# Transposes taken from a queue, one behind each wide product, in a hybrid decoder layer

## The chip, the cores and the metric

One core of a Trainium2 chip runs the whole layer. The metric is the device time of one execution in microseconds; three runs of each kernel are timed.

## The reference, cut to what matters

One layer for 2048 tokens behind 16 meta tokens, 1024 channels, four heads, in float32:

```
n = rmsnorm(h);  u, q, k, v = split(n @ w_in)
ya = pooling mixer of u (trailing means of 2, 4, 8, 16), w_pool
q, k = rmsnorm per head half (64 channels)
a  = softmax(q1 k1^T / 8) - lam * softmax(q2 k2^T / 8)      causal
yb = rmsnorm(a @ v) * 0.8
h  = h + [ya | yb] @ w_out
n  = rmsnorm(h);  u = n @ w_up            1024 x 5632
c  = causal depthwise conv of u (width 3) + b
h  = h + (silu(c_gate) * c_val) @ w_down
```

## The kernel before

Tokens go in 16 blocks of 128 (b = 0 to 15) and one of the 16 meta tokens (b = -1). Every float32 product is made from three products of split operands (hi with hi, hi with lo, lo with hi), which `mm3` writes out; each of them loads 128 columns of weights and streams 128 to 512 columns. A product here is called wide when it streams 256 or more.

TensorE contracts over partitions, so several operands are transposed first, each time 128 columns with the data as weights and the identity as what streams. A group of two to four such transposes fills one PSUM tile `pt`; then `split` empties it: ScalarE copies the hi part, VectorE subtracts to get lo. There are 1024 transposes, in four places:

- the norm's output `n` of each block, eight in two groups of four, by `transpose_split` (line 187) in the first stage. The result `nT` is used for head 0 and kept in DRAM for the other heads;
- q and k of each head and block, two, by `qk_store` (line 286). Their result goes by a transfer to `qk_d` in DRAM, and after every fourth block `load_kv` reads keys and values back;
- the mixed probabilities `p`, by `values` (lines 685 and 708), four to a group, for the products with v;
- the second norm's output `n`, eight by `out_finish` (line 987).

The stages: first, head 0's projection for all blocks together with the pooling mixer. Then attention of heads 0 to 3, score chunks (line 649, up to 512 keys) and products with v, woven with the projections of heads 1 to 3 and, for the last head, with the first half of the out projection. Then the second half of the out projection with the second norm, and behind it the feed-forward part, which holds more than half of the span. The first up-projection chunk, `first` (line 954, 72 products), is written ahead of the last `out_finish`.

A scheduler orders the instructions: each takes its place on its engine by its place in the program, by priorities, and by when the scheduler thinks that its operands are there. So products are used to fill what it takes for gaps. Transfers are all started by the queue SP in that order; one that waits holds up those behind it.

Of the kernel before, what the change touches and what calls it, by code (L numbers as in the profile page):

```python
# [76 lines left out]
def layer_kernel(  # L77
# [104 lines left out]
    def transpose_split(ps_pool, n, T, hi, lo):  # L182
        for half in range(2):
            pt = ps_pool.tile([P, 4, P], F32, name="pt")
            for j in range(4):
                kc = half * 4 + j
                nc.tensor.transpose(pt[:, j, :T], n[:T, kc * P:(kc + 1) * P], ident[:T, :T])  # L187
            split(pt[:, :, :T], hi[:, half * 4:half * 4 + 4, :T], lo[:, half * 4:half * 4 + 4, :T])
# [45 lines left out]
    def norm_block(b, ptr, g_row, h=None):  # L234
        T, pos = block(b)
        h = load_x(b) if h is None else h
        n = nrm.tile([P, D], F32, name="n")
        r = rms_rows(nrm, h[:T], T, "n1", n[:T])
        nc.vector.scalar_tensor_tensor(n[:T], h[:T], r, g_row[:T], ALU.mult, ALU.mult)
        pn, pc = pair_cols(b)  # L240
        if pn not in pairs:
            pairs[pn] = (nrm if pn % 2 else npa).tile([P, 2, KC, NM + 2 * P], F32R, name="nT", bufs=1)
        nT = pairs[pn][:, :, :, pc]
        transpose_split(ptr, n, T, nT[:, 0], nT[:, 1])
        nc.sync.dma_start(
            nT_d[b].rearrange("p a k t -> p (a k) t"),
            nT.rearrange("p a k t -> p (a k) t").bitcast(F32))
        return nT

    def qkv_block(h, b, nT, whi, wlo, ppm):  # L250
        T, pos = block(b)
        ps = ppm.tile([P, 512], F32, name="pm")
        mm3(ps[:T, :3 * P], [(nT[:, 0, kc, :T], nT[:, 1, kc, :T], whi[kc], wlo[kc]) for kc in range(KC)])
# [27 lines left out]
    def qk_store(h, b, qn, ps_pool, tag):  # L281
        T, pos = block(b)
        pt = ps_pool.tile([P, 4, P], F32, name=tag)
        qT = inp.tile([P, 2, 2, P], F32R, name="qT")
        for g in range(2):
            nc.tensor.transpose(pt[:, g, :T], qn[:T, g * P:(g + 1) * P], ident[:T, :T])
        split(pt[:, 0:2, :T], qT[:, :, 0, :T], qT[:, :, 1, :T])
        pn, pc = pair_cols(b)
        nc.sync.dma_start(
            qk_d[h][pn][:, :, :, pc].rearrange("p s a t -> p (s a) t"),  # L290
            qT[:, :, :, :T].rearrange("p s a t -> p (s a) t").bitcast(F32),
        )
# [98 lines left out]
    with tc.tile_pool(name="apm", bufs=4, space=PSUM, reuse_waits="tile") as ppm, \  # L391
# [44 lines left out]
        for b in range(-1, NB):  # L436
            nT = nTs.pop(0)
            if b == NB - 1:
                u_groups(NP - 1, (0, 1))
                u_groups(NP - 1, (2, 3))  # L440
# [186 lines left out]
    def scores(key, qs, n, ks, res):  # L627
        q0 = NM if n == 0 else 0
        for ib in range(2):
# [7 lines left out]
            for c in range(2):  # L637
                for ch in range(npc):
# [4 lines left out]
                    while c == 1 and live[1] >= P2_BUFS:  # L643
                        mix_next()
                    live[c] += 1
                    dst = ap.tile([P, 512], F32, name=f"p{c + 1}", bufs=P1_BUFS if c == 0 else P2_BUFS)[:, :k1 - k0]
                    pt[c].append(dst)
                    for a in range(2):
                        nc.tensor.matmul(  # L649
                            src, qs[:, c, a, q0 + ib * P:q0 + (ib + 1) * P], ks[:, c, k0:k1],  # L650
                            start=(a == 0), stop=(a == 1 and not diag))
                    if diag:
                        nc.tensor.matmul(
                            s_ps[:, k1 - k0 - P:k1 - k0], ident_bf, mask_bf, start=False, stop=True)
# [15 lines left out]
    def values(key, n, a, vs, vm):  # L670
# [18 lines left out]
        late = []  # L689

# [8 lines left out]
        for m in range(n + 1):  # L699
            pt = ptr.tile([P, 512], F32, name="pt")  # L700
            width = 512 if m < n else 3 * P
            for jj in range(2):
                j = 2 * m + jj
                for ib in range(2):
                    if j > 2 * n + ib:
                        continue
                    off = jj * QP + (ib if m < n or jj == 0 else 0) * P
                    nc.tensor.transpose(  # L708
                        pt[:, off:off + P], piece(a[ib], NM + j * P), ident)
            at = ap.tile([P, 2, 512], F32R, name="at", bufs=AT_BUFS)  # L710
            split(pt[:, :width], at[:, 0, :width], at[:, 1, :width])
            gone = [end for end in spans if end <= NM + 2 * (m + 1) * P]
            live[0] -= len(gone)
            spans = [end for end in spans if end > NM + 2 * (m + 1) * P]
            late.append((m, at))
            yield VLW * (1 - PSH)
            if len(late) > PV_LAG:
                products(*late.pop(0))
                yield VLW * PSH
        for m, at in late:  # L720
            products(m, at)
            yield VLW * PSH
# [52 lines left out]
    def project(h):  # L775
# [3 lines left out]

        def finish(b, qn):  # L780
            qk_store(h, b, qn, *((ppm, "pm") if QPM else (ptr, "pt")))
            if b > 0 and b % 4 == 3:
                part = b // 4
                if part == 0:
                    assert ended[0] >= (h - 1) * NP, (h, ended)
                    kvs[h] = alloc_kv(h)
                load_kv(h, part, kvs[h])
                parts.add((h, part))
# [11 lines left out]
        run_later(1 << 30)  # L800
        if h + 1 < H:
# [42 lines left out]
    def out_half(b, k0, base):  # L844
# [8 lines left out]
        for hf in range(2):  # L853
# [4 lines left out]
                for k in range(4)])  # L858
# [44 lines left out]
    def need(h, part):  # L903
        while (h, part) not in parts:
            if later:
# [13 lines left out]
    run_later(1 << 30)  # L919
    kv[1].release()  # L920
# [39 lines left out]
    with tc.tile_pool(name="os", bufs=2, **LEFT) as sp:  # L960
# [18 lines left out]
        def out_finish(b, n):  # L979
            T, pos = block(b)  # L980
            if b >= 7:
                n2T = sp.tile([P, KC, P], F32, name="n2T")
            for q in range(2):
                pt = ptr.tile([P, 512], F32, name="pt").rearrange("p (j t) -> p j t", t=P)
                for j in range(4):
                    kc = q * 4 + j
                    nc.tensor.transpose(pt[:, j, :T], n[:T, kc * P:(kc + 1) * P], ident[:T, :T])
                if b < 8:
                    t0 = max(0, pos - (NM - 4))
                    src = pt[:, :, T - 4:T] if b < 0 else pt  # L990
                    cols = slice(t0, t0 + (4 if b < 0 else T))
                    split(src, fnT[q][:, 0, :, cols], fnT[q][:, 1, :, cols])
                if b >= 7:
                    nc.scalar.copy(n2T[:, q * 4:q * 4 + 4], pt)  # L994
            if b >= 7:
                nc.sync.dma_start(n2_d[:, :, pos:pos + T].rearrange("k p t -> p k t"), n2T)
# [3 lines left out]
        for b in range(-1, NB):  # L1000
            n = out_block(b)
            if last is not None:
# [6 lines left out]
            last = (b, n)  # L1009
        first = up_products(0, load_up(0), ppx)  # L1010
        out_finish(*last)
    ppx.release()
# [122 lines left out]
```

## Time and profile before

| what | value |
|---|---|
| median of three runs | 2544.81 us (2540.98 to 2545.67) |
| span of the profiled execution | 2541.9 us |
| TensorE busy | 2492.5 us, 98% |
| VectorE, ScalarE, GpSimd busy | 62%, 37%, 16% |
| transfers | 314.32 MB, all on one core's 16 DMA engines |
| feed-forward part | from some 1060 us to the end |

The profiled execution is one more execution of the same program; of its time the profile gives the span from its first to its last instruction, and what lies around it is not shown. The span is 2.9 us below the median of the runs and inside their range. Times in rows are microseconds from the start of the span. Matmuls overlap and their ends are modelled, so the distance of two starts says what a product costs, not its duration.

### The profile page before, as it was taken

The page shows a single profiled execution, that of the slowest core. Times are in us where ns is not written, and L with a number is a line of the kernel's source. Part 1 is how long each engine was busy: PE and PEld are TensorE (multiplying, and loading weights), DVE is VectorE, ACT ScalarE, POOL GpSimd, SP SyncE. Part 2 cuts the span into 40 slices and gives each one's busy share as a digit, 9 for nine tenths or more (in the row PEclk, how much of TensorE's full clock was granted, in tenths as well). Part 3 has the DMA queues.
Part 4 walks back from the last instruction along what each step waited for, and adds up shares of the span by engine and source line. Part 5 has one row for each costly group of instructions (what it writes and reads, how often), then busy time and mean ns, then how long its engine had stood idle before and what let it go on. Part 6 is the DMA issues. An engine that isn't in the chain of part 4 may idle for free.

```text
span 2541.9 us, 35879 instructions
## 1 busy us (share of the span) xinstructions
PE 2492.5 (98%) x13614; PEld 2185.7 (86%) x13614; DVE 1564.3 (62%) x3106; ACT 948.0 (37%) x2270; POOL 410.5 (16%) x480
## 2 busy tenths in 40 slices
PE   8998999999989999999999999999999999999999
PEld 7997898888877887899999999998888888888887
DVE  7886898889798646454444444445554454445545
ACT  5544676667676434322221222223222122212221
POOL 1001555556575430000000000000000000000000
PEclk9999999999999999999999999999999999999999
DMA  9866767675655568911111111112611111111111
GB/s 274 257 204 202 216 202 213 202 225 175 226 159 159 188 197 273 292 55 48 42 34 50 50 50 50 42 50 83 207 50 42 50 50 37 39 50 50 50 34 66
DMA packets 320952, 314.32 MB, mean 124 GB/s; under 512 B 28188, under 2 KB 280012, under 8 KB 314636
## 3 DMA queue, kind: packets, MB, share of 16 engines
q1 hardware_dynamic: 320780, 312.03, 40.1%
q8 instruction: 107, 1.75, 0.3%
q14 instruction: 65, 0.53, 0.1%
HBM read 222.85 MB, written 89.13 MB: 123 GB/s over the span
## 4 chain that ended last, share of the span: by engine, by line
PE 90%; DMA 5%; DVE 3%; ACT 1%; issue 1%; POOL 0%; SPq 0%; ACTq 0%; DVEq 0%
PE pu L954 39%; PE pm L193 6%; PE pm L194 6%; PE pm L195 6%; PE pd L193 6%; PE pd L195 6%; PE pd L194 6%; PE s_ps L649 4%; PE pt L708 2%; DMA nTs<-nT_d 1%; PE o_ps L679 1%; PE o_ps L680 1%; PE o_ps L681 1%; DMA wraw<-in_w_in_dram 1%; PE pt L187 1%; PE pt L512 1%
## 5 line engine op out<-in xcount | busy, mean ns | idle before, releaser
L954 PE MATMUL pu<-fnT,uwh 128*128 128x344 f32 (+1 forms) x3520 | 807.1, 350 | 1.9 <-ACT n2T L994 1.9
L954 PEld LDWEIGHTS pu<-fnT,uwh 128*128 128x128 f32 x3520 | 617.6, 189 | 76.0 <-ACT n2T L994 2.1
L1090 DVE TENSOR_TENSOR acc<-pd,acc 128x512 f32<-128x512 f32 x368 | 252.8, 688 | 474.8 <-PE pd L195 474.4
L954 PE MATMUL pu<-fnT,uwl 128*128 128x344 f32 (+1 forms) x1760 | 453.7, 350 | 0.0
L179 ACT CAST uwh<-uraw 128x1024 fp32r<-128x1024 f32 x88 | 92.3, 1049 | 688.4 <-PE pu L954 677.3
L954 PEld LDWEIGHTS pu<-fnT,uwl 128*128 128x128 f32 x1760 | 312.0, 189 | 32.7
L193 PE MATMUL pd<-dwh,g 128*128 128x512 f32 x688 | 272.5, 396 | 3.0 <-DVE acc L1090 2.7
L195 PE MATMUL pd<-dwh,g 128*128 128x512 f32 x688 | 271.1, 394 | 0.0
L194 PE MATMUL pd<-dwl,g 128*128 128x512 f32 x688 | 270.9, 394 | 0.0
L656 ACT ACTIVATE p<-s_ps,nm 128x400 f32<-128x400 f32 (+4 forms) x352 | 211.6, 603 | 126.0 <-DVE nm L655 102.8
L180 DVE TENSOR_TENSOR uwl<-uraw,uwh 128x1024 fp32r<-128x1024 f32 x88 | 107.7, 1224 | 232.3 <-ACT uwh L179 230.5
L593 POOL TENSOR_SCALAR p<-p,fac 128x384 f32<-128x384 f32 (+4 forms) x164 | 219.5, 1353 | 102.9 <-DVE fac L588 72.9
L655 DVE TENSOR_REDUCE nm<-s_ps 128x1 f32<-128x400 f32 (+4 forms) x352 | 197.2, 566 | 57.0 <-PE s_ps L649 29.8
L649 PE MATMUL s_ps<-ks,qs 128*128 128x400 f32 (+4 forms) x704 | 196.3, 365 | 5.5 <-ACT p L656 3.6
L195 PEld LDWEIGHTS pd<-dwh,g 128*128 128x128 f32 x688 | 129.4, 188 | 30.9
L193 PEld LDWEIGHTS pd<-dwh,g 128*128 128x128 f32 x688 | 129.6, 188 | 29.9 <-DVE acc L1090 6.6
L193 PE MATMUL pm<-whi,nTs 128*128 128x384 f32 (+1 forms) x408 | 143.2, 353 | 10.4 <-DMA nTs<-nT_d 9.7
L194 PEld LDWEIGHTS pd<-dwl,g 128*128 128x128 f32 x688 | 129.3, 188 | 23.3
L179 ACT CAST g<-c 128x1026 fp32r<-128x1026 f32 (+1 forms) x44 | 46.2, 1050 | 261.5 <-DVE c L1070 162.0
L194 PE MATMUL pm<-wlo,nTs 128*128 128x384 f32 (+1 forms) x408 | 141.8, 348 | 0.1
L195 PE MATMUL pm<-whi,nTs 128*128 128x384 f32 (+1 forms) x408 | 141.4, 347 | 0.0
L649 PEld LDWEIGHTS s_ps<-ks,qs 128*128 128x128 f32 x704 | 117.0, 190 | 15.2 <-ACT p L656 8.2
(217 smaller groups left out, 4309.2 us busy)
## 6 DMA issues: line engine op xcount, KB each, us to landing
nTs<-nT_d SPq DMA_DIRECT2D x48, 1024.0 KB, 5.9
uraw<-in_w_up_dram SPq DMA_DIRECT2D x88, 512.0 KB, 3.9
draw<-in_w_down_dram SPq DMA_DIRECT2D x44, 512.0 KB, 4.0
nT_d<-nT SPq DMA_DIRECT2D x16, 1024.0 KB, 6.5
qk_d<-qT SPq DMA_DIRECT2D x64, 256.0 KB, 4.9
mt<-mix_d SPq DMA_DIRECT2D x32, 512.0 KB, 4.5
h_d<-xt SPq DMA_DIRECT2D x32, 512.0 KB, 5.2
qs<-qk_d SPq DMA_DIRECT2D x56, 256.0 KB, 4.4
```

The costliest lines, as they stand in the source:

```text
L179: nc.scalar.copy(hi, src)
L180: eng.tensor_tensor(lo, src, hi.bitcast(F32), ALU.subtract)
L193: nc.tensor.matmul(ps, a_hi, b_hi, start=(i == 0), stop=False)
L194: nc.tensor.matmul(ps, a_hi, b_lo, start=False, stop=False)
L195: nc.tensor.matmul(ps, a_lo, b_hi, start=False, stop=(i == n - 1))
L593: nc.gpsimd.tensor_scalar(a1, a1, fac[:, 0, ch:ch + 1], None, ALU.mult)
L649: nc.tensor.matmul(src, qs[:, c, a, q0 + ib * P:q0 + (ib + 1) * P], ks[:, c, k0:k1], start=(a == 0), stop=(a == 1 and not diag))
L655: nc.vector.tensor_reduce(nm[:, c, ch:ch + 1], src, AX.X, ALU.max, negate=True)
L656: nc.scalar.activation(dst, src, AF.Exp, bias=nm[:, c, ch:ch + 1], accum_out=ls[:, c, ch:ch + 1])
L708: nc.tensor.transpose(pt[:, off:off + P], piece(a[ib], NM + j * P), ident)
L954: nc.tensor.matmul(ps[:, bk, :wid], wt[:, kc], fnT[kc // 4][:, a, kc % 4, bk * w0:bk * w0 + wid], start=(kc == 0 and a == 0 and wt is wh), ...
L1090: nc.vector.tensor_tensor(acc[b][:, cs], ps, acc[b][:, cs], ALU.add)
```

## The change

Transposes are no longer issued where they are written. `turn` puts a group into the list `turning` with a function `end` for what follows it (the split, and the store or load behind that). `turn_one` issues the next transpose of the first group; the last of a group calls `end`. `mm3` with `wide` issues one behind each product: in the projections, in both halves of the out projection and, by a call of its own, behind each score product. With `tight` the next product is also tied behind that transpose for the scheduler; so it is for head 0's projection (`not h`) and the second half of the out projection (`k0 > 0`), not in attention. Places that need a result now empty the queue first (`turn_all`, `turned`).

```
+    def turn(pool, tag, steps, end):
+        group = dict(pool=pool, tag=tag, steps=list(steps), end=end, pt=None)
+        turning.append(group)
+        return group
+
+    def turn_one():
+        if turning:
+            group = turning[0]
+            if group["pt"] is None:
+                group["pt"] = group["pool"].tile([P, 512], F32, name=group["tag"])
+            out, in_, T = group["steps"].pop(0)
+            ins = nc.tensor.transpose(group["pt"][:, out:out + T], in_, ident[:T, :T])
+            if not group["steps"]:
+                turning.pop(0)
+                group["end"](group["pt"])
+            return ins
+        return None
...
-    def mm3(ps, pairs):
+    def mm3(ps, pairs, wide=False, tight=False):
...
-            nc.tensor.matmul(ps, a_hi, b_hi, start=(i == 0), stop=False)
-            nc.tensor.matmul(ps, a_hi, b_lo, start=False, stop=False)
-            nc.tensor.matmul(ps, a_lo, b_hi, start=False, stop=(i == n - 1))
+            for k, (a, b) in enumerate(((a_hi, b_hi), (a_hi, b_lo), (a_lo, b_hi))):
+                with tc.issue_after(turned.ins) if turned else nullcontext():
+                    ins = nc.tensor.matmul(ps, a, b, start=(i == 0 and k == 0), stop=(i == n - 1 and k == 2))
+                if wide:
+                    with tc.issue_after(ins.ins):
+                        turned = turn_one()
+                if not tight:
+                    turned = None
...
         for b in range(-1, NB):
             n = out_block(b)
+            turn_all()
             if last is not None:
                 out_finish(*last)
...
             last = (b, n)
+        turn_all()
         first = up_products(0, load_up(0), ppx)
         out_finish(*last)
+        turn_all()
```

In `values` the scores' PSUM and the p tiles (`live[0]`) are now given back when the group's last transpose is issued, and a score chunk that finds no free p tile issues transposes first.

What this makes of the order on the engines is seen at three places. The first is TensorE in head 0's projection, ahead of the products of a block (`pt<-ident,n` and `pt<-ident,qn` are transposes, `pm<-whi` and `pm<-wlo` products of the projection). Before:

```order
L187 MATMUL pt<-ident,n 128x128 x8
L286 MATMUL pt<-ident,qn 128x128 x2
L193 MATMUL pm<-whi_218,nT 128x384
L194 MATMUL pm<-wlo_219,nT 128x384
L195 MATMUL pm<-whi_218,nT 128x384
L193 MATMUL pm<-whi_223,nT 128x384
```

and in the change:

```order
L233 MATMUL pm<-whi_203,nT 128x384
L197 MATMUL pt<-ident,n 128x128
L233 MATMUL pm<-wlo_204,nT 128x384
L197 MATMUL pt<-ident,n 128x128
L233 MATMUL pm<-whi_203,nT 128x384
L197 MATMUL pt<-ident,n 128x128
L233 MATMUL pm<-whi_208,nT 128x384
L197 MATMUL pt<-ident,n 128x128
```

The eight and two transposes that stood ahead of the block's 24 products now stand behind its first ten products, one each.

The second is the queue SP where head 0 ends (`qk_d_7_82<-qT` is the last block's store of q and k, `nTs<-nT_d_60` the load of block 1 for head 1, `wraw` are weights of a later projection, `ks` reads the stored keys back, `qs` queries). Before:

```order
L217 DMA wraw<-in_w_in_dram 128x3x128 x3
L289 DMA qk_d_7_82<-qT 512x1x128
L794 DMA nTs<-nT_d_60 128x2048
L794 DMA nTs<-nT_d_61 128x2048
L307 DMA ks_360<-qk_d_7_82 64x2x256
L259 DMA v_d_108<-vt 16x256
L259 DMA v_d_108<-vt 128x256
L307 DMA ks_360<-qk_d_7_82 64x2x256
L544 DMA qs<-qk_d_2_77 64x2x512 x2
```

and in the change:

```order
L330 DMA qk_d_7_82<-qT 512x1x128
L260 DMA wraw<-in_w_in_dram 128x3x128
L352 DMA ks_330<-qk_d_7_82 64x2x256
L260 DMA wraw<-in_w_in_dram 128x3x128
L352 DMA ks_330<-qk_d_7_82 64x2x256
L593 DMA qs<-qk_d_2_77 64x2x512 x2
L853 DMA nTs<-nT_d_60 128x2048
```

The load of block 1 stood right behind the store; now two loads of ks, which wait for that store to land, and two of qs stand ahead of it, and two weight loads that stood before the store.

The third is TensorE at the end of the out projection (`pm<-ks,mt` and `pm<-vs,mt` are its products, `pu` those of the up projection; the last two groups of transposes are blocks 14 and 15). Before:

```order
L194 MATMUL pm<-vs_11323,mt 128x512
L195 MATMUL pm<-ks_11322,mt 128x512
L954 MATMUL pu<-fnT_13473,uwh 128x344 x3
L954 MATMUL pu<-fnT_13473,uwl 128x344 x3
L954 MATMUL pu<-fnT_13473,uwh 128x344 x3
L987 MATMUL pt<-ident,n_14431 128x128 x8
L954 MATMUL pu<-fnT_13473,uwh 128x344 x3
L954 MATMUL pu<-fnT_13473,uwl 128x344 x3
L954 MATMUL pu<-fnT_13473,uwh 128x344 x6
L954 MATMUL pu<-fnT_13473,uwl 128x344 x3
L954 MATMUL pu<-fnT_13473,uwh 128x344 x6
L954 MATMUL pu<-fnT_13473,uwl 128x344 x3
```

and in the change:

```order
L233 MATMUL pm<-vs_11300,mt 128x512
L233 MATMUL pm<-ks_11299,mt 128x512
L197 MATMUL pt<-ident,n_14431 128x128 x8
L197 MATMUL pt<-ident,n_14492 128x128 x8
L1017 MATMUL pu<-fnT_13472,uwh 128x344 x6
```

Between the last out product and the next chunk there were two bursts of eight with 9 and 24 up products around them; now there are the two bursts alone, and the 72 up products of that chunk stand earlier.

## Rows read from the trace of the kernel before

**Rows 1.** Table by stretches: window, its length, TensorE busy us (instructions), granted clock, DMA share, GB/s.

```profile
36.00:208.00 172.00, 172.00 (x1303) 1.00 0.82 239
...
250.00:712.00 462.00, 454.19 (x2857) 1.00 0.67 206
...
931.00:1060.00 129.00, 123.80 (x632) 1.00 0.83 259
```

**Rows 2.** List by line, TensorE: count | busy us, mean ns | idle before, releasers.

```profile
L708 PE MATMUL pt<-ident,p 128*128 128x128 f32 x544 | 85.6, 275 | 0.2
...
L187 PE MATMUL pt<-ident,n 128*128 128x128 f32 (+1 forms) x136 | 18.1, 275 | 10.1 <-DVE n L239 10.1
```

**Rows 3.** Timeline of TensorE, a burst of eight: start us, us, engine, line, operation.

```profile
1029.69 1.03 PE L987 MATMUL pt<-ident,n 128*128 128x128 f32 x8
1030.48 0.48 PE L194 MATMUL pm<-vs,mt 128*128 128x512 f32 x1
1030.80 0.39 PE L195 MATMUL pm<-ks,mt 128*128 128x512 f32 x1
```

**Rows 4.** Timeline of TensorE, a lone transpose in attention.

```profile
775.13 0.60 PE L649 MATMUL s_ps<-ks,qs 128*128 128x384 f32 x2
775.56 0.27 PE L708 MATMUL pt<-ident,p 128*128 128x128 f32 x1
775.59 0.47 PE L193 MATMUL pm<-ohi,mt 128*128 128x512 f32 x1
775.90 0.39 PE L194 MATMUL pm<-olo,mt 128*128 128x512 f32 x1
776.13 0.40 PE L195 MATMUL pm<-ohi,mt 128*128 128x512 f32 x1
```

**Rows 5.** Timeline of the queue SP, end of the first head.

```profile
223.93 0.56 SPq L289 DMA_DIRECT2D qk_d<-qT  x1
224.54 2.28 SPq L794 DMA_DIRECT2D nTs<-nT_d  x2
228.16 0.63 SPq L307 DMA_DIRECT2D ks<-qk_d  x1
...
230.81 1.23 SPq L544 DMA_DIRECT2D qs<-qk_d  x2
```

**Rows 6.** Timeline of TensorE, same place; in brackets the idle time before.

```profile
231.37 0.66 PE L193 MATMUL pm<-whi,nTs 128*128 128x384 f32 x1 [3.33 <-DMA nTs<-nT_d]
...
239.39 0.34 PE L194 MATMUL pm<-wlo,nTs 128*128 128x384 f32 x1
239.56 0.34 PE L195 MATMUL pm<-whi,nTs 128*128 128x384 f32 x1
```

**Rows 7.** Timeline of VectorE, last block of the out projection.

```profile
1050.87 0.69 DVE L859 TENSOR_TENSOR xt<-pm,xt 128x512 f32<-128x512 f32 x1 [2.03 <-PE pm L195]
...
1054.62 1.28 DVE L976 SCALAR_TENSOR_TENSOR n<-xt,n_r,g_row 128x1024 f32<-128x1024 f32 x1
```

**Rows 8.** Timelines of TensorE and ScalarE, same place.

```profile
1050.67 0.65 PE L954 MATMUL pu<-fnT,uwh 128*128 128x344 f32 x3
1051.15 0.64 PE L954 MATMUL pu<-fnT,uwl 128*128 128x344 f32 x3
...
1058.62 1.08 ACT L994 COPY n2T<-pt 128x512 f32<-128x512 f32 x2
...
1059.76 1.22 PE L954 MATMUL pu<-fnT,uwh 128*128 128x344 f32 x6 [1.91 <-ACT n2T L994]
```

**Rows 9.** Table by stretches: length, PE, PEld, DVE, ACT, POOL busy, clock, DMA share, GB/s.

```profile
231.40:237.00 5.60, 5.60 (x18) 5.60 (x19) 0.00 (x0) 0.00 (x0) 1.58 (x4) 0.50 0.92 275
```

**Rows 10.** Waits of TensorE, 250 to 931 us: us in total, times, longest.

```profile
PE pm L193 <- DMA nTs<-nT_d: 3.9, 2, 2.5
PE s_ps L649 <- ACT p L656: 3.3, 9, 0.7
...
PE pt L512 <- DVE ls L584: 0.4, 1, 0.4
```

More of the change, by code (lines that the diff above doesn't have):

```diff
@@ L1 @@
-from contextlib import ExitStack
+from contextlib import ExitStack, nullcontext
 import concourse.bass as bass
@@ L180, in split @@
         eng.tensor_tensor(lo, src, hi.bitcast(F32), ALU.subtract)
-    def transpose_split(ps_pool, n, T, hi, lo):
-        for half in range(2):
[L184 to L188, printed above, removed]
-    def mm3(ps, pairs):
+    turning = []
@@ new lines, in turned, with turn_all, transpose_split, done @@
+    def turned(group):
+        while any(g is group for g in turning):
+            turn_one()
+    def turn_all():
+        while turning:
+            turn_one()
+    def transpose_split(ps_pool, n, T, hi, lo, end):
+        for half in range(2):
+            ks = slice(half * 4, half * 4 + 4)
+            def done(pt, half=half, ks=ks):
+                pt = pt.rearrange("p (j t) -> p j t", t=P)
+                split(pt[:, :, :T], hi[:, ks, :T], lo[:, ks, :T])
+                if half:
+                    end()
+            turn(ps_pool, "pt", [(j * P, n[:T, (half * 4 + j) * P:(half * 4 + j + 1) * P], T)
+                                 for j in range(4)], done)
@@ L252, in qkv_block @@
         ps = ppm.tile([P, 512], F32, name="pm")
-        mm3(ps[:T, :3 * P], [(nT[:, 0, kc, :T], nT[:, 1, kc, :T], whi[kc], wlo[kc]) for kc in range(KC)])
+        mm3(ps[:T, :3 * P], [(nT[:, 0, kc, :T], nT[:, 1, kc, :T], whi[kc], wlo[kc]) for kc in range(KC)], True, not h)
         with tc.high_priority(offset=PRI_E):
@@ L279, in qkv_block, with qk_store, end @@
         return qn, sums, norm
-    def qk_store(h, b, qn, ps_pool, tag):
+    def qk_store(h, b, qn, ps_pool, tag, stored=None):
         T, pos = block(b)
[L283 to L287, printed above, removed]
-        pn, pc = pair_cols(b)
[L289 to L292, printed above, removed]
+        pn, pc = pair_cols(b)
+        def end(pt):
+            qT = inp.tile([P, 2, 2, P], F32R, name="qT")
+            split(pt.rearrange("p (j t) -> p j t", t=P)[:, 0:2, :T], qT[:, :, 0, :T], qT[:, :, 1, :T])
+            nc.sync.dma_start(
+                qk_d[h][pn][:, :, :, pc].rearrange("p s a t -> p (s a) t"),
+                qT[:, :, :, :T].rearrange("p s a t -> p (s a) t").bitcast(F32),
+            )
+            if stored:
+                stored()
+        turn(ps_pool, tag, [(g * P, qn[:T, g * P:(g + 1) * P], T) for g in range(2)], end)
     def alloc_kv(h):
@@ L644, in scores @@
                         mix_next()
+                    while c == 0 and live[0] >= P1_BUFS and turning:
+                        turn_one()
                     live[c] += 1
@@ L699, in values @@
         for m in range(n + 1):
-            pt = ptr.tile([P, 512], F32, name="pt")
             width = 512 if m < n else 3 * P
+            steps = []
             for jj in range(2):
@@ L707, in values, with end @@
                     off = jj * QP + (ib if m < n or jj == 0 else 0) * P
[L708 to L711, printed above, removed]
+                    steps.append((off, piece(a[ib], NM + j * P), P))
             gone = [end for end in spans if end <= NM + 2 * (m + 1) * P]
-            live[0] -= len(gone)
             spans = [end for end in spans if end > NM + 2 * (m + 1) * P]
-            late.append((m, at))
+            def end(pt, m=m, width=width, gone=len(gone)):
+                at = ats[m] = ap.tile([P, 2, 512], F32R, name="at", bufs=AT_BUFS)
+                split(pt[:, :width], at[:, 0, :width], at[:, 1, :width])
+                live[0] -= gone
+            late.append((turn(ptr, "pt", steps, end), m))
             yield VLW * (1 - PSH)
             if len(late) > PV_LAG:
-                products(*late.pop(0))
+                group, k = late.pop(0)
+                turned(group)
+                products(k, ats.pop(k))
                 yield VLW * PSH
-        for m, at in late:
-            products(m, at)
+        for group, k in late:
+            turned(group)
+            products(k, ats.pop(k))
             yield VLW * PSH
@@ L778, in project, with stored @@
         stages = []
-        def finish(b, qn):
[L781 to L788, printed above, removed]
+        def stored(b):
+            part = b // 4
+            if part == 0:
+                assert ended[0] >= (h - 1) * NP, (h, ended)
+                kvs[h] = alloc_kv(h)
+            load_kv(h, part, kvs[h])
+            parts.add((h, part))
+        def finish(b, qn):
+            qk_store(h, b, qn, ptr, "pt", (lambda: stored(b)) if b > 0 and b % 4 == 3 else None)
         for b in range(-1, NB):
@@ L904, in need @@
         while (h, part) not in parts:
-            if later:
+            if turning:
+                turn_one()
+            elif later:
                 later.pop(0)[1]()
```

44 lines of the change are left out of this document (25 added, 19 removed).

## The prediction

> **What bounds the kernel now.** The first view is the table by stretches, since a mean over the span mixes stages with different limits [rows 1]. From 36 to 208 us (first head's projections, pooling mixer) TensorE is busy all 172 us; from 250 to 712 us (attention with the next heads' projections) 454.2 of 462; from 931 to 1060 us (second half of the out projection) 123.8 of 129. The feed-forward part behind it is not edited. A busy matmul engine gains only from fewer or cheaper instructions, or where it stands idle. So there are two questions: does a transpose get cheaper behind a wide product, and which idle stretches come or go?
>
> The second view is the list of instructions by line: it shows 136 transposes of n on line 187 with 10.1 us of idle time, which is the wait for the first norm at the start, and 544 transposes of p on line 708 with 0.2 us [rows 2]. So once the kernel is under way the bursts wait for nothing, neither for data nor for a free PSUM tile. No such wait can be removed.
>
> **What a transpose costs in a burst and alone.** Starts are read, not durations, since matmuls overlap. In a burst of eight, the first starts at 1029.69, the next product at 1030.48, the product after it at 1030.80 [rows 3]. Two 512-wide products that follow each other are 0.23 us apart [rows 4], so the second gap, 0.32, holds 0.09 us that belong to the burst: 0.79 + 0.09 = 0.88 us, 110 ns for each of eight.
>
> The trace has transposes that already stand alone between wide products. At 775.56 one stands between 384-wide score products and a 512-wide out projection: 0.03 us to the next product, then 0.31 in place of 0.23, so 0.03 + 0.08 = 0.11 us [rows 4]. In such rows of two decimals the last digit is rounded; I take 114 ns for a lone one, 110 for a member of a burst. A lone transpose is not cheaper: it pays its 0.11 us wherever it stands.
>
> One rule speaks for the change and one against, both from the Trainium skill, "TensorE: Matmul & The Clock Gate". Its section "Step-by-step: what each phase is for" says that the next weights load while the present matmul runs; taken alone, a transpose behind a wide product would pay only its own stream. Its section "LDWEIGHTS (loading the stationary operand)" gives 128 columns at 1.2 GHz, so 107 ns as an estimate: the wide product behind a short transpose then shows its own load, and nothing is saved. By the second rule the price is near 0.11 us in both places, and the trace agrees with it.
>
> **The change part by part.** The number of instructions is the same on every engine. Counted in the order of instructions, the bursts are broken up in two of the three places only. In the first head's projection 22 runs of transposes become 121, of which 114 are single; in the second half of the out projection 20 become 122, of which 120 are single. In attention 230 runs become 224: there the products are not tied behind the transpose, and they stand in twos and fours as before.
>
> (a) *Price on TensorE.* 195 more runs at 4 ns (114 less 110) are +0.8 us. Bounds: nothing, and the first rival below.
>
> (b) *First head to second head.* The queue SP carries all transfers in order. In before, the last qk store of head 0 goes at 223.93 and the load of block 1 of nT right behind it at 224.54; only at 228.16 come the loads of ks, which wait for that store to land (4.2 us) [rows 5]. The product that needs this nT starts at 231.37 after 3.33 us of idle time [rows 6], 6.8 us after the issue. In the change the nT load stands behind the ks loads, the second pair of qs and two more weight loads (order, second place). ScalarE casts that qT two weight casts sooner, which I take as 2 us: store at 222, landed 226.2, then two ks at 0.63, a weight load at some 0.4 and two qs (1.23) [rows 5] make 229.1, plus 6.8 is 235.9, 4.5 us late. In between TensorE has seven more score chunks than before, 0.43 us each for a 384-wide one (775.13 to 775.56 [rows 4]), some 2.5 us over their sizes. Left: +2 us. Bounds: 0 (the store comes 5 us earlier, or the hole at the next block shrinks as much) and +5 (no chunk has its q in time, because the same qs loads are late).
>
> (c) *End of the out projection.* In before 33 up-projection products (9 and 24) stand behind the last out product. They hide the chain from that product to n2 of the last block: the last residual add at 1050.87, the norm's last step from 1054.62 for 1.28 us, so n is there at 1055.90, 5.23 us after the first of those products at 1050.67 [rows 7, 8]. In the change all 72 products of that chunk stand earlier, and behind the last out product come 16 transposes and then the next chunk. So TensorE does the first eight (0.88 us), waits for n until 5.2 us, does the other eight (to 6.1) and waits for their copies by ScalarE (0.6 us, half of 1.08 at 1058.62 [rows 8]): 6.8 us. In before the same way took 1059.76 - 1050.67 = 9.1 us, of which 33 products at 0.16 us (1050.67 to 1051.15 for three [rows 8]) are 5.3; without them 3.8. The hole costs 6.8 - 3.8 = +3.0 us, as those products ran at full speed in either place. What else is late: the clock. After the 3.33 us of idle time at 228 us the granted clock was 0.50 (1.2 of 2.4 GHz) for 5.6 us, in which 18 products of 384 columns took 0.31 us each [rows 9], in place of the 0.17 from 239.39 to 239.56 [rows 6]. The new hole is 4.3 us long, so I add +1.5 us. Bounds: +0.5 (earlier waits for mt and for the residual add are filled by the products moved forward) and +5.5 (the clock falls for as long as there: 18 x 0.14 = 2.5 us).
>
> (d) *Attention.* Runs are alike, the order is shuffled, and the transposes stand some microseconds later, as does the release of the p tiles. The named waits of TensorE from 250 to 931 us are nine rows and 14.3 us together, the largest nT loads with 3.9 and score products that wait for the exponential with 3.3 [rows 10]. I take 0 and keep -6 and +6, not half of 14.3 in either direction, because a new order draws new ones.
>
> Sum: 0.8 + 2 + 4.5 + 0 = +7 us. The profiled span is 2541.9, so 2549 in such an execution; the median of the runs is 2544.8, 2.9 more than that span, which makes 2551 to 2552. I say **2551**.
>
> **The rivals.** *1. A lone transpose is cheaper (faster).* A 512-wide product takes 0.23 us [rows 4], so a quarter, 58 ns, bounds the stream of 128 columns. If loads hid behind products, 234 transposes made single at 52 ns less would give -12 us, and with (b) and (c) 2539. For it: none of the lone ones seen stands in a strict alternation of one and one. Against it: 0.11 us at each. It decides below about 58 ns, where 234 x 52 ns outweigh the +7 and 5 us more; at 80 ns it would only cancel the +7. *2. No change.* The holes of (b) and (c) come, but the new order of attention gives back some 4 to 6 of its 14.3 us: 2546. For it: bursts that no longer block a score chunk. Against it: transposes wait for nothing there. *3. Worse attention.* Score chunks stand closer together in the new order, and three PSUM tiles must be emptied by a maximum and an exponential; if the 3.3 us of that wait become 10 and an nT load is late at each of the two later head changes, 2560.
>
> **How the numbers follow.** The sum's case 0.45 (its own range 2547 to 2557), no change 0.33, rival 1 and a lucky attention order together 0.15 (2536 to 2540), rival 3 0.07. The range 2539 to 2560 leaves out some 2 in 10. Runs of before differ by 0.2% (2540.98 to 2545.67), about what a measurement of this kernel can tell from no change; 0.2% is 5.1 us. Of the sum's case a fifth lies below 2549.9. So slower 0.43, same 0.41, faster 0.16.
>
> **What would show it.** Right: starts of a transpose and its product in head 0 sum to 0.28 to 0.29 us with a 384-wide product; an idle stretch of about 4 us ahead of the last eight transposes on the line that takes the place of 987, released by DVE; the product of block 1 of head 1 later than at 231.4. Wrong: 0.23 us for such a pair (rival 1); no idle stretch at the end of the out projection; or an attention stage that ends several us sooner.

## Result, and the profile after

The change made the kernel slower: 2582.57 us (median of four runs, 2581.01 to 2585.78) against 2545.24 us for the kernel before, timed beside it; ratio 1.0153, 95% interval 1.0139 to 1.0167. The prediction said slower as the likeliest, but 2551 us, at most 2560. The loss is 37 us by the medians and 40.1 us between the profiled spans.

The page of the kernel after, its span and TensorE's row; then the clock of the core in both kernels (after, before):

```profile
span 2582.0 us, 35866 instructions
PE 2515.9 (97%) x13614; PEld 2199.6 (85%) x13614; DVE 1566.7 (61%) x3106; ACT 954.8 (37%) x2270; POOL 415.0 (16%) x480
```
```profile
core 0: 2582.0 us, clock 0.987
```
```profile
core 0: 2541.9 us, clock 0.996
```

TensorE executes 13614 instructions in both, and no byte more is moved than the 314.32 MB of before. Its busy time rose from 2492.5 to 2515.9 us, +23.4; its idle time (span less busy) from 49.4 to 66.1, +16.7. Both make the 40.1. The mean granted clock says the same: 1.3% of 2582.0 less 0.4% of 2541.9 is some 23 us. So more than half of the loss is not waiting, but the slow clock after waits.

Where it lies is seen from the table by stretches, cut at the first score product, the first product of the second half of the out projection, and the first product of the down projection. Columns as in [rows 1], with the other engines between (PE, PEld, DVE, ACT, POOL busy, then clock, DMA share, GB/s). After:

```profile
36.00:208.00 172.00, 172.00 (x1292) 170.06 (x1291) 143.07 (x412) 87.37 (x254) 9.60 (x22) 1.00 0.79 234
...
223.60:956.70 733.10, 701.64 (x4182) 612.84 (x4181) 576.54 (x1578) 454.43 (x1464) 393.75 (x419) 0.97 0.62 191
...
956.70:1135.00 178.30, 167.21 (x853) 138.69 (x852) 85.54 (x158) 63.24 (x130) 3.14 (x4) 0.96 0.75 235
```

and before, with the same cuts:

```profile
224.20:931.40 707.20, 685.45 (x4178) 599.24 (x4176) 574.18 (x1577) 450.35 (x1464) 389.73 (x419) 0.99 0.64 197
...
931.40:1094.20 162.80, 157.60 (x845) 135.30 (x844) 84.82 (x157) 61.78 (x129) 3.44 (x4) 1.00 0.81 258
```

The first head and the feed-forward part are unchanged within 1 us. Attention took 25.9 us more (9.7 idle, 16.2 busy, most of that at the slower clock), the second half of the out projection 15.5 (5.9 idle, 9.6 busy, of which the clock, 0.96 against 1.00, makes some 7). What can follow a wait is seen in stretches ahead of and behind three holes of the kernel after:

```profile
301.50:306.00 4.50, 0.00 (x0) 0.00 (x0) 2.17 (x8) 1.56 (x5) 1.57 (x4) 0.89 0.92 323
306.07:310.50 4.43, 4.42 (x15) 4.43 (x16) 0.00 (x0) 0.00 (x0) 0.00 (x0) 0.50 0.54 178
...
388.25:390.80 2.55, 0.01 (x1) 0.00 (x0) 0.11 (x3) 0.51 (x1) 0.14 (x1) 0.90 0.64 129
390.80:393.00 2.20, 2.19 (x10) 2.14 (x11) 2.20 (x7) 2.17 (x8) 0.00 (x0) 0.50 0.21 66
...
419.56:420.90 1.34, 0.01 (x1) 0.01 (x1) 1.30 (x2) 0.69 (x2) 1.34 (x2) 1.00 0.22 75
420.90:423.00 2.10, 2.10 (x7) 2.10 (x8) 1.30 (x3) 0.00 (x0) 1.26 (x3) 0.53 0.05 15
```

After 4.50 us without a matmul, and also after 2.55 and 1.34 us, TensorE goes on at 1.2 in place of 2.4 GHz. The Trainium skill, "TensorE: Matmul & The Clock Gate", section "HAM oscillation — how this bites in real kernels", tells of a kernel whose matmuls wait for transfers in every round: each time they go on at the low clock, so the cost is paid again and again. The trace agrees behind the first and the third hole, which are waits for loads of nT; the second is a wait for a weight cast.

But not every wait of this length is followed by the slow clock. Two waits for loads of nT in the kernel before, each with a stretch behind it:

```profile
246.19:248.63 2.44, 0.00 (x0) 0.00 (x0) 2.38 (x12) 2.11 (x9) 0.00 (x0) 1.00 1.08 311
248.65:252.00 3.35, 3.35 (x19) 3.35 (x20) 0.40 (x3) 0.23 (x2) 0.00 (x0) 1.00 0.59 210
...
390.17:392.63 2.46, 0.00 (x0) 0.03 (x1) 2.46 (x10) 2.20 (x10) 0.60 (x1) 1.00 1.02 406
394.00:396.50 2.50, 2.50 (x10) 2.50 (x9) 0.59 (x1) 0.00 (x0) 2.50 (x4) 0.52 1.04 287
```

The first passes at the full clock, the second does not.

The waits of TensorE from 224 to 957 us, the largest rows (us in total, times, longest):

```profile
PE pm L233 <- DMA nTs<-nT_d: 8.6, 3, 4.6
PE s_ps L700 <- ACT p L708: 7.9, 16, 0.9
PE s_ps L700 <- DMA qs<-qk_d: 5.0, 2, 3.1
PE pm L233 <- ACT whi L179: 2.6, 1, 2.6
```

and before, from 224 to 931.4 us:

```profile
PE pm L193 <- DMA nTs<-nT_d: 9.7, 4, 3.3
PE s_ps L649 <- ACT p L656: 3.6, 10, 0.7
...
PE s_ps L649 <- DMA qs<-qk_d: 1.2, 1, 1.2
```

The score products' wait for the exponential more than doubled, and loads of qs and the weights' casts are late at head changes. The wait for loads of nT, though the largest row, is no longer than before. No single wait holds the loss.

### The profile page after: what moved, and what is told of

Same layout as the page of the kernel before. It is cut to its first block, busy times and chain, and to the rows that moved or that the text cites. A ratio compares the mean times of both kernels' runs of the same rounds, so it can differ in the third digit from the quotient of the medians.

```text
span 2582.0 us, 35866 instructions
## 1 busy us (share of the span) xinstructions
PE 2515.9 (97%) x13614; PEld 2199.6 (85%) x13614; DVE 1566.7 (61%) x3106; ACT 954.8 (37%) x2270; POOL 415.0 (16%) x480
## 2 busy tenths in 40 slices
DMA packets 320953, 314.32 MB, mean 122 GB/s; under 512 B 28189, under 2 KB 280013, under 8 KB 314637
## 4 chain that ended last, share of the span: by engine, by line
PE 89%; DMA 4%; DVE 4%; ACT 1%; issue 1%; POOL 0%; SPq 0%; DVEq 0%
PE pu L1017 38%; PE pm L233 20%; PE pd L233 18%; PE s_ps L700 4%; PE pt L197 3%; PE o_ps L732 1%; PE o_ps L731 1%; PE o_ps L733 1%; DMA nTs<-nT_d 1%; DMA wraw<-in_w_in_dram 1%; DMA mt<-mix_d 1%; DVE nm L707 1%; ACT p L708 0%; DMA qs<-qk_d 0%; DVE p L648 0%
## 5 line engine op out<-in xcount | busy, mean ns | idle before, releaser
L233 PE MATMUL pd<-dwh,g 128*128 128x512 f32 x1376 | 484.6, 395 | 2.3 <-DVE acc L1155 2.0
L233 PE MATMUL pm<-whi,nTs 128*128 128x384 f32 (+1 forms) x816 | 234.9, 352 | 16.9 <-DMA nTs<-nT_d 8.6
L233 PEld LDWEIGHTS pm<-whi,nTs 128*128 128x128 f32 (+1 forms) x816 | 147.8, 189 | 23.9 <-ACT whi L179 7.4
L180 DVE TENSOR_TENSOR at<-pt,at 128x512 fp32r<-128x512 f32 (+2 forms) x176 | 106.5, 607 | 23.3 <-ACT at L179 23.0
L648 DVE SCALAR_TENSOR_TENSOR p<-p,fac,p 128x384 f32<-128x384 f32 (+4 forms) x164 | 116.9, 716 | 2.9 <-POOL p L642 2.6
```

What stands on the lines that cost most here:

```text
L180: eng.tensor_tensor(lo, src, hi.bitcast(F32), ALU.subtract)
L233: ins = nc.tensor.matmul(ps, a, b, start=(i == 0 and k == 0), stop=(i == n - 1 and k == 2))
L648: nc.vector.scalar_tensor_tensor(a1, pt[1][ch], fac[:, 1, ch:ch + 1], a1, ALU.mult, ALU.add)
```

## Experiments

Theories at the start. *A*: idle time and clock, from operands that come late in the new order. *B*: a lone transpose costs far more than one in a burst. For all experiments the queue got a switch for each place; a group of a place that is off is issued at once where it is written, as in the kernel before:

```
+QUEUED = ("head0", "qk", "p", "out")
...
-    def turn(pool, tag, steps, end):
+    def turn(pool, tag, steps, end, place):
         group = dict(pool=pool, tag=tag, steps=list(steps), end=end, pt=None)
-        turning.append(group)
+        if place in QUEUED:
+            turning.append(group)
+        else:
+            pt = pool.tile([P, 512], F32, name=tag)
+            for out, in_, T in group["steps"]:
+                nc.tensor.transpose(pt[:, out:out + T], in_, ident[:T, :T])
+            end(pt)
         return group
```

All results, with lengths of the two stages (cut as above) in the one profiled execution of each:

| run | median us | ratio to before, 95% | attention | out projection |
|---|---|---|---|---|
| before (profile shown) | 2545.24 | | 707.2 | 162.8 |
| full change | 2582.57 | 1.0139 to 1.0167 | 733.2 | 178.4 |
| only_head0 | 2544.92 | 1.0003 to 1.0025 | 708.2 | 161.3 |
| only_qk | 2547.70 | 1.0004 to 1.0032 | 711.1 | 160.9 |
| only_p | 2545.01 | 0.9993 to 1.0016 | 707.0 | 161.6 |
| only_out | 2552.48 | 1.0032 to 1.0070 | 708.4 | 173.3 |
| qk_and_p | 2567.59 | 1.0070 to 1.0112 | 728.2 | 171.3 |
| head0_and_out | 2554.95 | 1.0033 to 1.0066 | 707.3 | 174.8 |
| all_but_head0 | 2580.82 | 1.0130 to 1.0164 | 726.6 | 181.9 |
| qk_ahead | 2558.77 | 1.0052 to 1.0082 | 722.4 | 163.4 |
| qk_priority | 2545.06 | 0.9999 to 1.0018 | 707.2 | 163.5 |
| p_and_late_qk | 2563.68 | 1.0060 to 1.0099 | 713.2 | 170.8 |
| out_held | 2554.97 | 1.0035 to 1.0071 | 711.6 | 169.4 |
| out_untied | 2542.80 | 0.9987 to 1.0005 | 711.3 | 160.7 |
| out_three_mt | 2555.41 | 1.0032 to 1.0062 | 712.4 | 167.1 |
| qk_and_p_later_loads | 2566.45 | 1.0067 to 1.0100 | 723.1 | 173.2 |
| late_qk_alone | 2548.16 | 1.0016 to 1.0036 | 718.4 | 164.2 |
| qk_end_priority | 2565.39 | 1.0074 to 1.0113 | 724.2 | 168.9 |
| all_with_priority | 2568.37 | 1.0075 to 1.0109 | 714.7 | 183.8 |
| all_priority_untied | 2558.26 | 1.0045 to 1.0098 | 709.2 | 170.2 |

Before, timed beside each set, had medians of 2542.62 to 2543.96. A stage length comes from one execution: before, only_out, out_held and out_untied have the same program up to the end of attention, and their attention took 707.2 to 711.6 us. In qk_and_p and qk_and_p_later_loads TensorE runs the same instructions in the same order, and attention took 728.2 and 723.1. Differences of some 5 us in these columns are nothing.

### One place at a time

`QUEUED = ("head0",)`, `("qk",)`, `("p",)` and `("out",)`.

> Queue on in the first head's projection alone, bursts everywhere else. Theory A (the loss is idle time and the slow clock behind it, from late loads in attention and late operands at the end of the out projection): the pairs in the first head cost what a burst costs, so only the head junction moves: +0 to +4 us, 2545 to 2549. Theory B (a transpose alone costs much more than one in a burst; 38 us over 234 single ones is 0.16 us each): 114 single ones give +18 us, 2563.

> Queue on for the transposes of q and k of heads 1 to 3 alone. Theory A: these transposes now stand behind others, their stores go later, the loads of keys behind them hold up the queue of transfers, and the products that need a block of nT wait: +5 to +15 us, 2550 to 2560. Theory B: the transposes stand in pairs as before, so 0, 2545.

> Queue on for the transposes of the probabilities alone. Theory A: a new order of attention in which the nT loads meet other work: +5 to +15 us, 2550 to 2560; that the q and k part costs most (their stores hold up the transfer queue) would leave this one under +5. Theory B: they stand in twos and fours as before, so 0, 2545.

> Queue on in the second half of the out projection alone. Theory A: the idle stretch ahead of the last eight transposes (4.3 us), its slow clock, and some waits for residual and mixer tiles that the ties do not let other products fill: +8 to +12 us, 2553 to 2557. Theory B: 120 single transposes at 0.16 us give +19 us, 2564. The sum as predicted for this part alone: +5, 2550.

B falls at once: 114 single transposes in the first head cost 0.14% with the junction, where B wanted 18 us. For A the surprise is attention: q and k alone cost 0.18%, p alone 0.05%. The four ratios add up to 0.88%, the full change lost 1.53%. So places act together.

### Two and three places

`("qk", "p")`, `("head0", "out")` and `("qk", "p", "out")`. Theory A1: q and k stand in one queue behind groups of p; A2: parts add up.

> Queue on for q, k and the probabilities of attention, bursts in the first head and in the out projection. Theory A1 (one queue: the pairs of q and k stand behind groups of probabilities that wait for their mix, so stores, key loads and nT loads go late; it needs both kinds in the queue): +18 to +28 us, 2562 to 2572, with two or more waits of over 2.5 us for nT loads. Theory A2 (parts add up: +4.6 for q and k alone, +1.2 for the probabilities alone): +6 us, 2550.

> Queue on in the first head and in the out projection, bursts in attention. If the parts add up (0.14% and 0.51% measured alone): +16 us, 2560; in the full change the rest, 23 us, is then attention's. If the loss needs the first head's queue and the out projection's together: 2575 or more.

> Queue on everywhere but in the first head. Theory A1: 2575 to 2580, since the first head costs 3 us at most. If the first head's queue is what spoils attention (its stores come out at other times, so attention starts in another order): 2560 or less.

A2 falls: q, k and p together cost 0.91% where they alone make 0.23%. The first head and the out projection together cost no more than their sum (0.49% against 0.65%), and without the first head nearly all of the loss stays (1.47%). So there are two parts: q and k with p in attention, and the out projection by itself; 0.91% and 0.51% make 1.42%.

### Why q and k with p cost

`qk_store` of before ran in `run_later`, under `tc.high_priority(offset=PRI_L)`; a transpose that `turn_one` issues behind a product has lost that raised priority with the scheduler. Theory A3 says that this is what costs, A4 that the stores are late for any reason. Three edits of qk_and_p or only_p; the third raises a lag counted in ticks, steps of the loop that weaves attention with the projections:

```
         if place in QUEUED:
-            turning.append(group)
+            at = len(turning)
+            while place == "qk" and at and turning[at - 1]["pt"] is None:
+                at -= 1
+            turning.insert(at, group)
```
```
     def turn_one():
...
+        with tc.high_priority(offset=PRI_L) if group["place"] == "qk" else nullcontext():
             if group["pt"] is None:
                 group["pt"] = group["pool"].tile([P, 512], F32, name=group["tag"])
             out, in_, T = group["steps"].pop(0)
             ins = nc.tensor.transpose(group["pt"][:, out:out + T], in_, ident[:T, :T])
```
```
-QS = (2, 4, 7)
+QS = (2, 4, 9)
```

> As qk_and_p, but a group of q and k is put into the queue ahead of all groups that are not begun. Theory A1 (q and k are late because they stand behind groups of probabilities): the +24 us of qk_and_p fall to +8 or less, 2544 to 2552. Theory A3 (it is not the place in the queue, but that these transposes and what follows them have lost the raised priority with which the scheduler took them before): no change, 2562 to 2572.

> As qk_and_p, but the transposes, splits and stores of q and k have the raised priority back that their burst had; their place in the queue stays. Theory A3: back to +8 or less, 2544 to 2552. Theory A1: still +15 to +25, 2559 to 2569, as the scheduler cannot take them before the program has written them.

> As only_p, with the transposes of q and k in bursts outside the queue and with raised priority, but written two ticks later (the third lag 9 in place of 7), which puts them as far behind their block as in qk_and_p (4.35 score chunks on average, against 4.31 there and 3.95 in only_p). Theory A4 (that the stores are late is the cause, whatever makes them late): +15 to +25, 2559 to 2569. Theory A1 or A3 (place or priority): +5 or less, 2544 to 2549.

Priority alone takes the loss away: 0.09% in place of 0.91%, with the place in the queue unchanged. The edit raises the transposes and all that follows them. A place further ahead gives back only a part (0.67%, between the two ranges). But A4 isn't wrong either: q and k in bursts and with priority, only written two ticks later, cost 0.80%. Attention in qk_and_p, by stretch and by its largest waits:

```profile
223.50:951.70 728.20, 692.52 (x4153) 600.07 (x4152) 573.62 (x1575) 453.18 (x1462) 390.94 (x419) 0.98 0.62 191
```
```profile
PE pm L239 <- DMA nTs<-nT_d: 11.4, 5, 4.1
PE s_ps L706 <- ACT p L714: 7.0, 17, 1.0
PE s_ps L706 <- DMA qs<-qk_d: 6.9, 1, 6.9
```

and in qk_priority (edits shift the line numbers):

```profile
223.30:930.50 707.20, 686.34 (x4163) 597.87 (x4161) 574.46 (x1576) 451.26 (x1463) 386.94 (x419) 0.99 0.63 197
```
```profile
PE pm L240 <- DMA nTs<-nT_d: 5.4, 4, 3.4
PE s_ps L707 <- ACT p L715: 4.1, 12, 0.7
PE s_ps L707 <- DMA qs<-qk_d: 3.1, 1, 3.1
```

Idle time is 35.7 us in the one and 20.9 in the other; 12.7 of these 14.8 us are the three rows' difference, and busy time differs by 6.2 for nearly the same work. The waits for nT and for the exponential are many short ones; the one for queries is a single hole of 6.9 us. The kernel before, as fast as qk_priority, has 9.7, 3.6 and 1.2 us in these rows: against it the growth is in the exponential and the queries, and the row of nT tells little.

Three more runs asked by which way. In the first, loads of keys and values are written one block later, so that the transfer queue needn't stand still for the store just issued:

```
+        waiting = []
+        def flush(b=None):
+            while waiting:
+                stored(waiting.pop(0))
+            if b is not None and b > 0 and b % 4 == 3:
+                waiting.append(b)
...
         def finish(b, qn):
-            qk_store(h, b, qn, ptr, "pt", (lambda: stored(b)) if b > 0 and b % 4 == 3 else None)
+            qk_store(h, b, qn, ptr, "pt", lambda: flush(b))
```

> As qk_and_p with its order of chunks, but the loads of keys and values are written one block later, behind the next block's store, so that the queue of transfers need not stand still for the store just issued. The queue waited 69.5 us for stores of q and k in qk_and_p (56.8 before, 38.9 in only_p). If this standstill is how late stores cost time: the wait falls under 45 us and the time to 2544 to 2555. If not: 2562 or more.

The edit missed its aim. The queue's wait, 205 to 760 us, is still:

```profile
SPq L358 <- DMA qk_d<-qT: 66.8, 23, 5.6
```

so the run, at 0.83%, says nothing on that way. The second delays q and k in the kernel before; the third raises the priority of `group["end"]` alone, the splits, the store and the loads behind it.

> The kernel before with the transposes of q and k written two ticks later (third lag 9), in bursts, priority kept, nothing queued. If lateness costs by itself: +10 to +20, 2554 to 2564. If it takes the other order of chunks, in which p_and_late_qk lost 0.8%: +5 or less, under 2549, like only_qk (0.18%).

> As qk_and_p, with raised priority for the splits and the store behind the transposes of q and k, but not for the transposes. If the transposes' late place on TensorE is what costs: +15 to +25, 2559 to 2569. If it is the splits and stores, late behind other work of ScalarE, VectorE and the transfer queue: back to +8 or less, under 2552.

In the order of before, two ticks cost 0.26%; in the order that queued p brings, 0.75% (0.80 less 0.05). And priority behind the transposes gives nothing back (0.94%), so the transposes themselves must be taken early too. A run with the transposes alone raised is missing.

How late q and k are can be read from the traces. For the 51 blocks of heads 1 to 3, this is the mean time from the copy of a block's q and k out of PSUM (`qn<-pm`) to the issue of their store (`qk_d<-qT`), beside the idle time of TensorE in attention, in the one profiled execution of each:

| run | copy to store, us | idle, us | time over before |
|---|---|---|---|
| qk_priority | 29.3 | 20.9 | 0.09% |
| only_p | 29.5 | 20.6 | 0.05% |
| before | 29.7 | 21.8 | |
| p_and_late_qk | 30.4 | 27.2 | 0.80% |
| qk_end_priority | 30.5 | 30.2 | 0.94% |
| late_qk_alone | 30.8 | 27.5 | 0.26% |
| only_qk | 30.9 | 25.7 | 0.18% |
| qk_ahead | 31.3 | 33.6 | 0.67% |
| full change | 31.4 | 31.5 | 1.53% |
| qk_and_p | 31.7 | 35.7 | 0.91% |

Late stores and idle time go together, and the two runs that move nothing but the lag (p_and_late_qk against only_p, late_qk_alone against before) both gain some 6 us of idle time. Single steps in this table count for little: the program of before gave 21.8 to 23.6 us of idle time in four executions, and the same order on TensorE 35.7 and 30.2 in qk_and_p and qk_and_p_later_loads. But its two ends are clear. That speaks for A4, with lost priority as what makes the stores late. The times don't follow in step: only_qk and late_qk_alone are as late and hardly lose. By which way lateness costs, and why more of it costs with p queued, stays open.

### The out projection

```
                 for bk in range(nbk):
+                    with tc.issue_after(behind.ins) if behind and kc >= 4 else nullcontext():
...
-        first = up_products(0, load_up(0), ppx)
+        first = up_products(0, load_up(0), ppx, ends[0])
```

`ends[0]` is the last out product. The other edits of only_out: `True, k0 > 0` becomes `True, False` in `out_half` (out_untied), and `mt` gets `bufs=3` (out_three_mt).

> As only_out, but the second half of the first up projection chunk (36 of 72 products) is tied behind the last out product, where 33 stood before the change. If the loss of only_out (0.5%, of which some 9 us fall in the last 25 us of that stage) is the missing cover of the second norm: the idle stretch ahead of the last eight transposes goes, and the time is +2 to +4 us, 2546 to 2549. If it is the ties in the blocks before: 2552 or more, as there is less to fill their waits with.

> As only_out, but the next product is not tied behind its transpose, so that the scheduler places them; 5 and 24 up products stand around the two bursts at the end again and 20 transposes stay single. If the ties cost (+13 us by the interval, +9 by the medians): 2543 to 2548. If it is the queue itself, that the transposes come a block's length later: 2552 or more.

> As only_out with a third buffer for the mixer tiles mt, so that their loads can be issued one block sooner. The waits for mt in the out projection were 4.4 us in only_out against 1.4 before. If late mt loads are what the ties expose: they fall to 1.5 us and the time to 2548 or less than only_out by 3 to 5 us; the idle stretch of 4.1 us ahead of the last eight transposes stays. If the queue of transfers (it waits for residual loads) is what holds them, a third buffer changes nothing: 2552 to 2556.

Stretch and waits of that stage in only_out:

```profile
928.90:1102.10 173.20, 163.09 (x845) 135.76 (x844) 85.72 (x157) 62.68 (x129) 3.44 (x4) 0.98 0.78 242
```
```profile
PE pm L239 <- DMA mt<-mix_d: 4.4, 4, 1.9
PE pt L203 <- DVE n L1045: 4.1, 1, 4.1
```

in out_held:

```profile
934.70:1104.00 169.30, 161.76 (x846) 134.41 (x844) 85.56 (x157) 62.76 (x129) 3.44 (x4) 0.99 0.78 248
```
```profile
PE pm L239 <- DMA mt<-mix_d: 4.1, 3, 2.4
PE pu L1027 <- ACT n2T L1064: 1.9, 1, 1.9
```

in out_untied:

```profile
935.30:1096.00 160.70, 156.84 (x846) 135.05 (x845) 85.02 (x157) 62.95 (x129) 3.44 (x4) 1.00 0.81 261
```
```profile
PE pm L239 <- DMA mt<-mix_d: 1.9, 2, 1.7
PE pu L1023 <- ACT n2T L1060: 1.9, 1, 1.9
```

With 36 up products held back, the 4.1 us wait for n is gone, as expected, but the time isn't better (0.53% against 0.51%): the mt waits stay, one of them now 2.4 us, and the stage's clock is 0.99. The two intervals are some 10 us wide, so a gain of a few us isn't excluded, but the 2546 to 2549 us of the first theory are. Without the ties the whole loss is gone (-0.04%, interval 0.9987 to 1.0005), and the mt waits fall from 4.4 to 1.9 us. With a third buffer for mt its waits leave the list and the stage took 167.1 us in the profile, yet the time didn't follow (2555.41). So the order that the ties force costs, and the wait for n is only one of the places where it shows.

### Both causes together

> The full change with raised priority for the transposes, splits and stores of q and k in attention. If that priority is the attention stage's loss: the +38 us fall to the out projection's +11 and the first head's +2, 2555 to 2559. If the parts of the change act together in another way: 2565 or more.

> The full change with raised priority for q and k in attention and without the ties in the second half of the out projection. If these two are the whole of the loss: 2543 to 2549, about even with before (the first head's +0.14% stays). If the order of the whole is worse for other reasons: 2556 or more. Nothing says that it could be faster than before by over 0.2%.

With priority attention falls from 733.2 to 714.7 us and the loss to 0.92%; 2568.37 us lies in the second range, not in 2555 to 2559. Without the ties as well the stages are 709.2 and 170.2, and the loss is 0.72% in place of 1.53%; 2558.26 is again in the second range. So what takes each loss away alone takes away only about half of it in the whole change.

In the profiled execution attention is nearly as long as before; some 7 us stay in the second half of the out projection, though its ties are gone (waits for mt 3.5 us, for the residual add 2.1). Four of the six kernels with slow attention and nothing queued in the out projection show that too (168.9 to 173.2 us; qk_ahead and late_qk_alone do not). Here attention was not slow, so that link doesn't explain it. The execution profiled, 2551.43 us, is also the fastest of the four; where the 7 us between it and the median lie, no profile shows. The rest of the loss stays open. The single times of this kernel, 2551 to 2565 us, lie wider than those of any other.

## Why the prediction was wrong, step by step

**(a) Price of a transpose: right.** Starts in the first head after the change:

```profile
99.69 0.42 PE L233 MATMUL pm<-whi,nT 128*128 128x384 f32 x1
99.95 0.27 PE L197 MATMUL pt<-ident,n 128*128 128x128 f32 x1
99.98 0.42 PE L233 MATMUL pm<-wlo,nT 128*128 128x384 f32 x1
100.23 0.27 PE L197 MATMUL pt<-ident,n 128*128 128x128 f32 x1
100.26 0.42 PE L233 MATMUL pm<-whi,nT 128*128 128x384 f32 x1
```

A pair takes 0.57 / 2 = 0.285 us, the product 0.17 of it, so the transpose 0.11 to 0.12, in a strict alternation too. The first rival (58 ns) is out.

**(b) First head to second: place right, size lost in the scatter.** The product of block 1 of head 1 starts at 237.18 us, not 231.37 (5.8 us late where 4.5 was said). Its own wait for nT is gone; others stand there instead, 3.68 us for a weight cast and 1.94 for queries:

```profile
221.69 0.82 PE L233 MATMUL pm<-whi,nTs 128*16 128x384 f32 x2 [3.68 <-ACT whi L179]
...
234.22 1.43 PE L700 MATMUL s_ps<-ks,qs 128*128 128x272 f32 x4 [1.94 <-DMA qs<-qk_d]
237.18 0.66 PE L233 MATMUL pm<-whi,nTs 128*128 128x384 f32 x1
```

The +2 us fit only_head0 (1 to 6 us by its interval).

**(c) End of the out projection: mechanism right, term too small.** The hole came as worked out, the wait for n and then the short one for its copies (against [rows 7, 8]):

```profile
1096.22 1.34 PE L197 MATMUL pt<-ident,n 128*128 128x128 f32 x8 [4.09 <-DVE n L1039]
1098.24 2.09 PE L1017 MATMUL pu<-fnT,uwh 128*128 128x344 f32 x6 [0.67 <-ACT n2T L1054]
```

Predicted were some 4.3 and 0.6. But the term was +4.5 us and the stage lost 15.5 (10.5 in only_out): idle time rose by 5.9 where 3.0 was said, busy time by 9.6 where 1.5 was said for the clock. What it left out are waits for mt (1.4 us before, 4.4 after) and for the residual add (1.6), and the clock behind them. My lower bound let the products that moved forward fill earlier waits. With half of them put back, out_held lost the wait for n and kept 4.1 us of waits for mt, and its time stayed. Without the ties the loss was gone: the cause is the order that the ties force, not the missing cover alone.

**(d) Attention: the step that failed.** I took 0 with bounds of -6 and +6, because transposes stood in runs as before and "a new order draws new" waits. It was +26 us. I saw that the transposes "stand some microseconds later" and gave that no price. What makes those of q and k late was in the code: they moved out of a region of raised priority into a queue without it. Queued alone they cost 0.18%; with p queued too, 0.91%. That both are needed, and that priority on the transposes and what follows repairs it there, is shown. That lateness is what costs is supported by the two runs with the longer lag, not proved; why the order that queued p brings is so much more sensitive is not known. And in the whole change the repair of both parts gives back about half (0.72% stays).

**The rivals.** The third had the right sign and place: the exponential's wait rose to 7.9 us (10 was said), and loads of queries were late at head changes; those of nT in total were not. It was priced at 2560, since it counted waits and not the slow clock: attention gained 16.2 us of busy time on 9.7 of idle time. The second, no change, is out.

**The range** ended at 2560. The upper ends of the four terms together (0.8, 5, 5.5 and 6) make 2562, so it wasn't only that they weren't added: (d) was bounded by idle time alone, and (c) by the clock behind one hole. That the time would rise was said for (b) and (c), which made less than half of the loss; the larger part came from the term put at nothing.

## What to carry to other kernels

Before a burst is broken up, measure a lone instruction of it: here it cost the same 0.11 us, so there was nothing to win. When work moves from where it was written into a queue, look at what it leaves behind: a raised priority, an early place, fillers that a tie no longer lets in; none of that shows in instruction counts. And price a wait of a busy TensorE twice, without and with the slow clock behind it: over this change 16.7 us of idle time came with 23.4 us of busy time, but a wait of 2.44 us in the kernel before passed without.

No version tried beats the kernel before; only_p, qk_priority and out_untied, each with its own places queued, are level with it.

## What was not expected of the hardware

That idle stretches as short as 1.34 and 2.55 us stood ahead of a granted clock of 0.50 to 0.53. In the kernel before I had read it after one of 3.33 us alone [rows 6, 9], though its trace shows it after 2.46 us as well. After 2.44 us the clock stayed at 1.00, so the length of a wait alone doesn't say whether it falls; what else does, these runs don't show.
